# Stick-breaking mixer of a decoder trunk: projection with features on the partitions, and token factors on the scores

## The chip, the cores and the metric

The kernel runs on one core of a Trainium2 chip. The metric is the device time of one execution in microseconds, the median of three runs. TensorE (PE) does the matmuls and the transposes, VectorE (DVE), ScalarE (ACT) and GpSimd (POOL) the rest, and SyncE (SP) issues most DMAs. Inputs and outputs are fp32.

## The reference, cut to what matters

Two layers, 512 tokens, 1024 features. Each layer is half a feed-forward step, three token mixers A, B and C that share one input projection, gates and an output projection, and another half of a feed-forward step. The change lies in mixer C, which has six heads of 64 features:

```python
u = rms_norm(h, g_mix)
proj = u @ w_in
c = c_in.reshape(B, S, 3, C_HEADS, HEAD_DIM)             # query, key, value
o_c = stick_breaking_attention(c[:, :, 0], c[:, :, 1], c[:, :, 2])
...
z = einsum('bqhd,bshd->bhqs', qb, k) * dh ** -0.5
before = s_pos < tb                                       # strictly causal
log_1mb = where(before, log_sigmoid(-z), 0.0)
between = cumsum(log_1mb, axis=3, reverse=True) - log_1mb
a = where(before, exp(log_sigmoid(z) + between), 0.0)
o = einsum('bhqs,bshd->bqhd', a, vf)
```

The weight of a key is sigmoid(z) times the product of sigmoid(-z) over all keys between it and the query.

## The kernel before

**Numbers.** TensorE reads values in a rounded fp32 form (F32R). A value that must be exact is held as two such parts: `hi`, a copy by ScalarE that rounds, and `lo`, which VectorE gets by subtracting `hi` from the value. A product of two values is three matmuls: hi x hi, hi x lo and lo x hi. For the normalised input the parts are `gh` and `gl` (eight tiles of 128 features by 512 tokens each), for the weights `whi` and `wlo`. A transpose is a matmul with the identity `ident`, and runs in plain fp32.

**Normalisation.** `gh` and `gl` hold the input times the gain `g`, without the division by the root mean square, which belongs to the token. `rstd` computes that factor with tokens on the partitions: `r` (and `rq` = r/8, with the scale of the scores in it), a column per block of 128 tokens. `rbcast` spreads it over a tile `Rb` of 128 partitions by 512 tokens, for results that have features on the partitions. Both are called while the projection for the first pair of mixer C runs (`after`).

**The stream.** Weights go through the core as a sequence of jobs (`mix_jobs`, and `side_jobs` when the first has nothing ready). A job yields chunks: `fetch` starts the chunk's load on SP's queue and its splits in `wsplit` (L346-362: `raw` has three buffers, `whi` and `wlo` four), one chunk ahead of the one that `step` runs. Its `use` issues the matmuls into accumulator banks (`acc`, four banks).

**The units.** The attention work is cut into units: Python generators that yield the time after which they want to be resumed. `weave` keeps a model clock, to which every matmul and transpose adds its cost, resumes the units that are due and fills up with steps of the stream. So TensorE's queue, which keeps the order of the program, has projection matmuls with pieces of attention strewn in. On the other engines the scheduler of the framework may reorder what is ready.

**Mixer C.** Heads go in pairs (`p` = 0, 1, 2). `c_inputs` projects query, key and value of a pair: `project_in` with tokens on the partitions, four accumulators (one for each block of 128 tokens) of 384 columns (128 each for query, key and value), in four chunks of two K tiles. The stationary operand is the input, the moving one the weights. When a block is done, `evac` copies it out: `cq` (times `rq`), `ck` (times `r`, each head twice side by side, so that the transposes give it on both halves of the partitions), and `v_split` takes the value with its factor apart into `hi` and `lo`. `c_prep` is a unit that turns key and query round: for each head `k_dup` transposes four blocks of `ck` (tile `tps`) and splits the result in `kh` and `kl`; `q_stacks` transposes four blocks of `cq` and makes one tile `qs` per head, with the high part on one half of the partitions and the low part on the other. A score is then two matmuls (`scores`): `qs` against `kh` and against `kl`.

`c_unit` is one attention unit, half of a head's queries. Its `chain` goes from the scores (bank `sps`, one buffer): two sigmoids on ScalarE, of the scores for `e` and of their negative for `f`; a causal select on GpSimd after each; on VectorE a scan of `f` from the right with products; on GpSimd the product of `e` and the scanned `f`. After `chain.delay` TensorE transposes `e` (bank `tps`, two buffers) and it is split into `ph`/`pl` or `pzh`/`pzl`, and multiplied with the value's parts into the bank `ops`. The order in `mix_units` is: the preparation of pair 0, two units, the preparation of pair 1, two units, and so on; in the last pair the two of mixer B, `b_keys` and `b_compress`, take the place of a preparation.

Of the kernel before, what the change touches and what calls it, by code (L numbers as in the profile page):

```python
# [8 lines left out]
F32 = mybir.dt.float32  # L9
F32R = mybir.dt.float32r  # L10
I32 = mybir.dt.int32
AF = mybir.ActivationFunctionType
ALU = mybir.AluOpType
# [4 lines left out]
KD = D // 128  # L18
# [3 lines left out]
C_IN0 = A_IN + 512 + 768 + 24  # L22
# [33 lines left out]
class Trunk:  # L56
# [237 lines left out]
    def rstd(self, dil=False):  # L294

        nc = self.nc
        ps = self.tps()
        n = 8 if dil else 4
        ssd = self.ss.rearrange("p (m c) -> p c m", c=4)
        for j in range(n):  # L300
            rows = ssd[:, j - 4, :] if j > 3 else self.ss[:, j * 128:(j + 1) * 128]
            self.mm(ps[:, j:j + 1], rows, self.ones[:, 0:1], start=True, stop=True)
        tile_ = lambda name: self.rp.tile([128, 8], F32, tag=name, name=name, bufs=2)[:, :n]
        ms, r, t, rq = tile_("ms"), tile_("r"), tile_("rt"), tile_("rq")
        nc.vector.tensor_scalar(ms, ps[:, 0:n], 1.0 / D, EPS, op0=ALU.mult, op1=ALU.add)
        nc.scalar.activation(r, ms, AF.Sqrt)
        nc.vector.reciprocal(r, r)
        nc.vector.tensor_tensor(t, ms, r, op=ALU.mult)
        nc.vector.tensor_tensor(t, t, r, op=ALU.mult)
        nc.vector.tensor_scalar(t, t, -0.5, 1.5, op0=ALU.mult, op1=ALU.add)  # L310
        nc.vector.tensor_tensor(r, r, t, op=ALU.mult)
        if dil:
            nc.vector.tensor_scalar(rq, r, 0.125, None, op0=ALU.mult)
        self.r, self.rq = r, rq

    def rbcast(self):
# [375 lines left out]

    def q_stacks(self, view):

        nc = self.nc
        ps = self.trans4(view)
        out = []
        for h in range(2):
            t = self.st(F32R, "qs")
            own = slice(64 * h, 64 * h + 64)  # L700
            oth = slice(64 - 64 * h, 128 - 64 * h)
            nc.scalar.activation(t[own], ps[own], AF.Copy)
            nc.vector.tensor_tensor(t[oth], ps[own], t[own].bitcast(F32), op=ALU.subtract)
            out.append(t)
        return out
# [94 lines left out]


    def c_inputs(self, l, p):
        nc = self.nc
        c = self.cin[p] = {}

        def pre():
            if p == 0:
                self.begin_mix(l)
            elif p == 1:
                self.dilate()  # L810
            c["nq"] = self.mp.tile([128, 4, 128], F32, tag="oh", name="cq", bufs=5)
            c["nk"] = self.mp.tile([128, 4, 256], F32, tag="nat", name="ck", bufs=2)
            c["v"] = self.mp.tile([128, 4, 2, 128], F32R, tag="v2", name="v2", bufs=3)

        def evac(j, ps):
            r, rq = self.r[:, j:j + 1], self.rq[:, j:j + 1]
            nc.scalar.activation(c["nq"][:, j, :], ps[:, 0:128], AF.Copy, scale=rq)
            nc.scalar.activation(
                c["nk"][:, j, :].rearrange("p (h r d) -> p h r d", h=2, r=2),
                ps[:, 128:256].rearrange("p (h d) -> p h d", h=2)[:, :, None, :].to_broadcast([128, 2, 2, 64]),  # L820
                AF.Copy, scale=r)
            self.v_split(c["v"], j, ps[:, 256:384], 2, r)

        return self.project_in(l, [(C_IN0 + t * 384 + p * 128, 128) for t in range(3)], 2, False, evac, pre,
                               lambda: self.done.add(("c", l, p)),
                               after=(None, None, lambda: self.rstd(True), self.rbcast) if p == 0 else ())

    def c_prep(self, l, p):
        def make(U):
            c = self.cin[p]  # L830
            c["k"] = []
            yield "", 1300
            for h in range(2):
                c["k"].append(self.k_dup(lambda j: c["nk"][:, j, 128 * h:128 * h + 128]))
                yield "", 2000
                if h == 0:
                    c["q"] = self.q_stacks(lambda j: c["nq"][:, j, :])
                    yield "", 2000
            self.done.add(("cp", l, p))

        return Unit(make, need=lambda: ("c", l, p) in self.done)

    def c_unit(self, l, p, h, u):
        nc = self.nc

        def chain(i, S_, e):
            n = 128 * (i + 1)
            f = self.et("f")[:, :n]
            for t, sgn, fill in ((f, -1.0, 1.0), (e, 1.0, 0.0)):
                nc.scalar.activation(t, S_, AF.Sigmoid, scale=sgn)  # L850
                nc.gpsimd.affine_select(t[:, i * 128:], t[:, i * 128:], pattern=[[-1, 128]], compare_op=ALU.is_gt,
                                        fill=fill, base=0, channel_multiplier=1)
            nc.vector.tensor_tensor_scan(f[:, ::-1], f[:, ::-1], f[:, ::-1], 1.0, op0=ALU.mult, op1=ALU.min)
            nc.gpsimd.tensor_tensor(e[:, 0:n - 1], e[:, 0:n - 1], f[:, 1:n], op=ALU.mult)  # L854

        chain.delay = (4500, 4900)

        def make(U):
            c = self.cin[p]

            def first(O):
                if u == 0:
                    O["t"] = self.ops()
                    O["new"] = True

            def end(O):
                if u == 1:
                    if h == 0:
                        c["of"] = self.mp.tile([128, 512], F32, tag="of", name="of", bufs=1)
                    self.head_out(O["t"], h, c["of"])  # L870
                    O["free"] = self.clock + 2500
                    if h == 1:
                        self.oc.append(self.o_split(c["of"]))
                        self.done.add(("co", l, p))
                        if p == 2:
                            self.done.add(("cdone", l))

            yield from self.attend(U, u, c["q"][h], c["k"][h], chain, c["v"], h, self.O, u == 0, first, True, end)

        return Unit(make, need=lambda: ("cp", l, p) in self.done, gap=4500 if u else 3000, tiles=4 if u else 3,  # L880
                    pt=True)
# [844 lines left out]
```

## Time and profile before

| | value |
| --- | --- |
| median of three runs | 2807.02 us (2807.02, 2805.44, 2807.44) |
| the profiled execution | 2808.57 us, of which the span is 2806.9 us |
| granted TensorE clock, mean | 0.997 |
| PE busy | 2772.0 us, 99% |
| DVE busy | 1498.6 us, 53% |
| ACT busy | 1176.3 us, 42% |
| POOL busy | 486.2 us, 17% |
| DMA | 274.57 MB, mean 98 GB/s |

Matmuls overlap in the trace: a matmul of 512 columns has an entry of 0.39 us, and they start 0.23 us apart. Busy time of PE is therefore not the sum of its rows, and the cost of one more matmul is read from the distance of the starts. The chain of work that ended last shows this distance, since each of its pieces reaches to the start of the next. In the first layer mixer C's first query block (`cq`) is copied out at 398.4 us, in the second layer the last one at 1829.4 us.

### The profile page before, as it was taken

To read this page: it belongs to the slowest core of one execution; us is meant where nothing else is said; L and a number is where in the kernel's file an instruction comes from. 1 tells how busy PE (TensorE), PEld (TensorE's weight loads), DVE (VectorE), ACT (ScalarE), POOL (GpSimd) and SP (SyncE) were. 2 spreads that over 40 slices of the span, in tenths; PEclk is the share of its full clock that TensorE was granted. 3 is DMA by queue.
4 is the path that set the end of the run, shared out by engine and by line. 5 is a ranking of instruction groups with operands and counts; after the bars stand their busy time and mean duration, and the time that the engine had idled before them with its cause. 6 is when DMAs were issued, how large, how long until landed. Compare 5 with 4: busy or idle time off the path is not lost.

```text
span 2806.9 us, 39062 instructions
## 1 busy us (share of the span) xinstructions
PE 2772.0 (99%) x14281; PEld 2385.3 (85%) x14281; DVE 1498.6 (53%) x2983; ACT 1176.3 (42%) x2427; POOL 486.2 (17%) x577
## 2 busy tenths in 40 slices
PE   8999999999999999999999999999999999999998
PEld 7888898889989888888888888988899898888886
DVE  5464356567655674544354443565767456645433
ACT  4333246455644433333233332554656444433332
POOL 2121012122301231110011100221333012311100
PEclk9999999999999999999999999999999999999999
DMA  3332332332233243332333333323222333333332
GB/s 129 98 96 92 117 95 83 99 93 83 67 107 101 87 150 98 98 95 94 98 97 98 98 102 107 94 90 99 86 78 79 102 106 109 120 102 95 97 98 75
DMA packets 298575, 274.57 MB, mean 98 GB/s; under 512 B 14616, under 2 KB 278928, under 8 KB 298384
## 3 DMA queue, kind: packets, MB, share of 16 engines
q1 hardware_dynamic: 291744, 261.34, 30.6%
q10 hardware_dynamic: 6640, 10.75, 1.1%
q8 instruction: 112, 1.84, 0.3%
q14 instruction: 79, 0.65, 0.1%
HBM read 253.69 MB, written 18.35 MB: 97 GB/s over the span
## 4 chain that ended last, share of the span: by engine, by line
PE 95%; DVE 2%; issue 1%; POOL 1%; ACT 1%; DMA 0%; ACTq 0%; DVEq 0%; POOLq 0%
PE acc L82 66%; PE tps L82 9%; PE sps L82 8%; PE ops L82 8%; PE tps L102 4%; DVE wlo L359 0%; DMA gt<-gate 0%; POOL e L854 0%; POOL ss L292 0%; POOL ra L678 0%; DVE e L1227 0%; DMA gr<-in_cmp_pe_v_dram 0%; ACT e L1229 0%; PE acc L102 0%; DVE rb L679 0%
## 5 line engine op out<-in xcount | busy, mean ns | idle before, releaser
L359 DVE TENSOR_TENSOR wlo<-raw,whi 128x512 fp32r<-128x512 f32 (+3 forms) x944 | 650.4, 695 | 866.9 <-ACT whi L358 844.7
L358 ACT ACTIVATE whi<-raw 128x512 fp32r<-128x512 f32 (+3 forms) x944 | 561.5, 601 | 1043.6 <-PE acc L82 765.2
L82 PE MATMUL acc<-gh,whi 128*128 128x512 f32 x928 | 364.3, 393 | 0.0
L82 PE MATMUL acc<-gh,wlo 128*128 128x512 f32 x928 | 361.6, 390 | 0.0
L82 PE MATMUL acc<-gl,whi 128*128 128x512 f32 x928 | 361.4, 389 | 0.0
L530 POOL TENSOR_TENSOR a<-a,Rb 128x512 f32<-128x512 f32 x88 | 130.0, 1503 | 907.4 <-DVE a L529 893.5
L82 PE MATMUL acc<-hh,whi 128*128 128x512 f32 x704 | 274.2, 390 | 0.0
L82 PE MATMUL acc<-hh,wlo 128*128 128x512 f32 x704 | 273.9, 389 | 0.0
L82 PE MATMUL acc<-hl,whi 128*128 128x512 f32 x704 | 273.9, 389 | 0.0
L82 PEld LDWEIGHTS acc<-gh,wlo 128*128 128x128 f32 x928 | 174.1, 188 | 36.7
L82 PEld LDWEIGHTS acc<-gl,whi 128*128 128x128 f32 x928 | 174.4, 188 | 34.9
L82 PEld LDWEIGHTS acc<-gh,whi 128*128 128x128 f32 x928 | 174.4, 188 | 34.7
L82 PE MATMUL acc<-whi,gh 128*128 128x384 f32 (+2 forms) x576 | 203.1, 353 | 0.0
L82 PE MATMUL acc<-wlo,gh 128*128 128x384 f32 (+2 forms) x576 | 197.7, 343 | 0.5 <-DVE wlo L359 0.5
L82 PE MATMUL acc<-whi,gl 128*128 128x384 f32 (+2 forms) x576 | 197.2, 342 | 0.0
L82 PEld LDWEIGHTS acc<-hh,wlo 128*128 128x128 f32 x704 | 132.1, 188 | 27.5
L82 PEld LDWEIGHTS acc<-hh,whi 128*128 128x128 f32 x704 | 132.1, 188 | 27.4
L82 PEld LDWEIGHTS acc<-hl,whi 128*128 128x128 f32 x704 | 132.1, 188 | 27.1
L82 PE MATMUL acc<-whi,gd 128*128 128x384 f32 x384 | 134.6, 350 | 0.0
L82 PE MATMUL acc<-wlo,gd 128*128 128x384 f32 x384 | 129.3, 337 | 0.0
L82 PE MATMUL acc<-whi,gld 128*128 128x384 f32 x384 | 129.1, 336 | 0.0
L82 PE MATMUL tps<-gh,whi 128*128 128x512 f32 x320 | 124.5, 389 | 0.0
(377 smaller groups left out, 5412.6 us busy)
## 6 DMA issues: line engine op xcount, KB each, us to landing
raw<-in_ffn_w_dram SPq DMA_DIRECT2D x256, 512.0 KB, 3.4
raw<-in_w_in_dram SPq DMA_DIRECT2D x288, 128.0 KB, 2.3
raw<-in_w_gate_dram SPq DMA_DIRECT2D x48, 512.0 KB, 3.5
raw<-in_w_in_dram SPq DMA_DIRECT2D x16, 512.0 KB, 3.6
raw<-in_w_out_dram SPq DMA_DIRECT2D x16, 512.0 KB, 3.5
gate<-gt ACTq DMA_DIRECT2D x28, 256.0 KB, 2.0
gt<-gate SPq DMA_DIRECT2D x28, 256.0 KB, 2.8
raw<-in_w_up_dram SPq DMA_DIRECT2D x16, 384.0 KB, 3.0
```

Of the source, the lines that this page charges most:

```text
L82: self.nc.tensor.matmul(out, lhsT, rhs, start=start, stop=stop, **kw)
L102: self.nc.tensor.transpose(out, in_, self.ident[:n, :n])
L358: nc.scalar.activation(hi, x, AF.Copy)
L359: nc.vector.tensor_tensor(lo, x, hi.bitcast(F32), op=ALU.subtract)
L530: nc.gpsimd.tensor_tensor(v[j], v[j], self.Rb, op=ALU.mult)
```

## The change

Mixer C's projection puts the features on the partitions. The weights are now the stationary operand and `gh`/`gl` (512 tokens) the moving one; each pair has three accumulators of 512 columns, in the order value, query, key, in the same four chunks of two K tiles. All three go through the same chunks; value and query are finished and copied out a little ahead of the key.

- The query's accumulator already has the layout of `qs`: `stack_q` (the second half of the old `q_stacks`) splits it straight from the bank. It carries no factor.
- The key's accumulator is multiplied by `Rb` on VectorE into `ck` (in SBUF, 128 features by 512 tokens); `post` then writes `kh` and `kl` of each head on both halves of the partitions, four pairs of operations on 64 partitions, out of `ck`.
- The value is copied to `cv`; `c_prep` transposes its four blocks and calls `v_split` on them with `r`. That is all that `c_prep` still does.
- The query's factor stands now in the sigmoids: `scale` is a column, `rq` for `e`, and for `f` the new `nrq` = -r/8 that `rstd` computes.

```diff
--- before.py
+++ after.py
@@ -310,7 +310,9 @@
         nc.vector.tensor_scalar(t, t, -0.5, 1.5, op0=ALU.mult, op1=ALU.add)
         nc.vector.tensor_tensor(r, r, t, op=ALU.mult)
         if dil:
+            self.nrq = tile_("nrq")
             nc.vector.tensor_scalar(rq, r, 0.125, None, op0=ALU.mult)
+            nc.vector.tensor_scalar(self.nrq, r, -0.125, None, op0=ALU.mult)
         self.r, self.rq = r, rq
 
     def rbcast(self):
@@ -692,8 +694,10 @@
 
     def q_stacks(self, view):
 
-        nc = self.nc
-        ps = self.trans4(view)
+        return self.stack_q(self.trans4(view))
+
+    def stack_q(self, ps):
+        nc = self.nc
         out = []
         for h in range(2):
             t = self.st(F32R, "qs")
@@ -800,42 +804,81 @@
 
 
     def c_inputs(self, l, p):
+
         nc = self.nc
         c = self.cin[p] = {}
+        W = self.ins["w_in"][l]
+        starts = [C_IN0 + t * 384 + p * 128 for t in (2, 0, 1)]
+        after = {2: lambda: self.rstd(True), 3: self.rbcast} if p == 0 else {}
+        ps = []
 
         def pre():
             if p == 0:
                 self.begin_mix(l)
             elif p == 1:
                 self.dilate()
-            c["nq"] = self.mp.tile([128, 4, 128], F32, tag="oh", name="cq", bufs=5)
-            c["nk"] = self.mp.tile([128, 4, 256], F32, tag="nat", name="ck", bufs=2)
             c["v"] = self.mp.tile([128, 4, 2, 128], F32R, tag="v2", name="v2", bufs=3)
-
-        def evac(j, ps):
-            r, rq = self.r[:, j:j + 1], self.rq[:, j:j + 1]
-            nc.scalar.activation(c["nq"][:, j, :], ps[:, 0:128], AF.Copy, scale=rq)
-            nc.scalar.activation(
-                c["nk"][:, j, :].rearrange("p (h r d) -> p h r d", h=2, r=2),
-                ps[:, 128:256].rearrange("p (h d) -> p h d", h=2)[:, :, None, :].to_broadcast([128, 2, 2, 64]),
-                AF.Copy, scale=r)
-            self.v_split(c["v"], j, ps[:, 256:384], 2, r)
-
-        return self.project_in(l, [(C_IN0 + t * 384 + p * 128, 128) for t in range(3)], 2, False, evac, pre,
-                               lambda: self.done.add(("c", l, p)),
-                               after=(None, None, lambda: self.rstd(True), self.rbcast) if p == 0 else ())
+            c["vt"], kt = (self.mp.tile([128, 512], F32, tag="oh", name=n, bufs=5) for n in ("cv", "ck"))
+            return kt
+
+        def evac(j):
+            if j == 0:
+                nc.scalar.activation(c["vt"], ps[0], AF.Copy)
+            else:
+                c["q"] = self.stack_q(ps[1])
+
+        def post(kt):
+            nc.vector.tensor_tensor(kt, ps[2], self.Rb, op=ALU.mult)
+            c["k"] = []
+            for h in range(2):
+                own, oth = (slice(64 * x, 64 * x + 64) for x in (h, 1 - h))
+                hi, lo = self.st(F32R, "kh"), self.st(F32R, "kl")
+                for rows in (own, oth):
+                    nc.scalar.activation(hi[rows], kt[own], AF.Copy)
+                    nc.vector.tensor_tensor(lo[rows], kt[own], hi[own].bitcast(F32), op=ALU.subtract)
+                c["k"].append((hi, lo))
+            self.done.add(("c", l, p))
+
+        def entries():
+            kt = []
+            for ci in range(4):
+                def use(hi, lo, ci=ci):
+                    if ci == 0:
+                        kt.append(pre())
+                        ps.extend(self.acc() for _ in range(3))
+                    for j in range(3):
+                        cs = slice(j * 128, (j + 1) * 128)
+                        for k in range(2):
+                            g = 2 * ci + k
+                            self.mm(ps[j], hi[k][:, cs], self.gh[g], start=(g == 0), stop=False)
+                            self.mm(ps[j], hi[k][:, cs], self.gl[g], start=False, stop=False)
+                            self.mm(ps[j], lo[k][:, cs], self.gh[g], start=False, stop=(g == KD - 1))
+                            if k == 0:
+                                yield 0
+                        if ci == 3 and j < 2:
+                            evac(j)
+                        if j < 2:
+                            yield 0
+                    if ci in after:
+                        after[ci]()
+                    if ci == 3:
+                        post(kt[0])
+                    yield 1
+
+                rows = slice(ci * 256, ci * 256 + 256)
+                yield [(j * 128, 128, W[rows, c0:c0 + 128]) for j, c0 in enumerate(starts)], 2, 384, use
+
+        return None, entries()
 
     def c_prep(self, l, p):
+
         def make(U):
             c = self.cin[p]
-            c["k"] = []
             yield "", 1300
-            for h in range(2):
-                c["k"].append(self.k_dup(lambda j: c["nk"][:, j, 128 * h:128 * h + 128]))
-                yield "", 2000
-                if h == 0:
-                    c["q"] = self.q_stacks(lambda j: c["nq"][:, j, :])
-                    yield "", 2000
+            ps = self.trans4(lambda j: c["vt"][:, j * 128:(j + 1) * 128])
+            for j in range(4):
+                self.v_split(c["v"], j, ps[:, j * 128:(j + 1) * 128], 2, self.r[:, j:j + 1])
+            yield "", 2000
             self.done.add(("cp", l, p))
 
         return Unit(make, need=lambda: ("c", l, p) in self.done)
@@ -846,8 +889,8 @@
         def chain(i, S_, e):
             n = 128 * (i + 1)
             f = self.et("f")[:, :n]
-            for t, sgn, fill in ((f, -1.0, 1.0), (e, 1.0, 0.0)):
-                nc.scalar.activation(t, S_, AF.Sigmoid, scale=sgn)
+            for t, rq, fill in ((f, self.nrq, 1.0), (e, self.rq, 0.0)):
+                nc.scalar.activation(t, S_, AF.Sigmoid, scale=rq[:, i:i + 1])
                 nc.gpsimd.affine_select(t[:, i * 128:], t[:, i * 128:], pattern=[[-1, 128]], compare_op=ALU.is_gt,
                                         fill=fill, base=0, channel_multiplier=1)
             nc.vector.tensor_tensor_scan(f[:, ::-1], f[:, ::-1], f[:, ::-1], 1.0, op0=ALU.mult, op1=ALU.min)
```

Three places, as the engines' queues have them. First ScalarE, from the end of the projection of pair 0 in the first layer up to the first sigmoid of the first unit, which loads its table first. Before:

```order
L818 ACTIVATE ck<-acc,r 128x256
L725 ACTIVATE v_2977<-acc,r 128x2x64
L323 ACTIVATE Rb<-tps 128x512
L358 ACTIVATE whi<-raw 128x384 x2
L712 ACTIVATE kh<-tps 128x512
L358 ACTIVATE whi<-raw 128x384 x2
L702 ACTIVATE qs<-tps 64x512 x2
L712 ACTIVATE kh<-tps 128x512
L358 ACTIVATE whi<-raw 128x384 x2
L850 ACT_TABLE_LOAD
L850 ACTIVATE f<-sps 128x128
```

After (`cv` is the value's copy, `ck` the key in SBUF, `v_` the value's parts):

```order
L826 ACTIVATE cv<-acc 128x512
L706 ACTIVATE qs<-acc 64x512
L360 ACTIVATE whi<-raw 128x384 x2
L706 ACTIVATE qs<-acc 64x512
L325 ACTIVATE Rb<-tps 128x512
L837 ACTIVATE kh<-ck 64x512 x4
L729 ACTIVATE v_2975<-tps,r 128x2x64
L360 ACTIVATE whi<-raw 128x384 x2
L729 ACTIVATE v_2975<-tps,r 128x2x64 x2
L893 ACT_TABLE_LOAD
L893 ACTIVATE f<-sps,nrq 128x128
L729 ACTIVATE v_2975<-tps,r 128x2x64
```

The key's splits have moved from the preparation, where they came one head at a time between the weights' `whi`, into one row of four right behind `Rb`; the value's splits, which stood in the projection's end, are now between and behind the weights' `whi` and beside the first sigmoids.

Second VectorE, at the end of the projection of pair 1 (the two rows L853, after L896, are the scans of a unit of pair 0; `pzl` and `pl` are low parts of its transposed weights). Before:

```order
L853 SCALAR_TENSOR_TENSOR f<-f 128x384
L853 SCALAR_TENSOR_TENSOR f<-f 128x512
L359 TENSOR_TENSOR wlo<-raw,whi 128x384 x2
L713 TENSOR_TENSOR kl<-tps,kh 128x512
L766 TENSOR_TENSOR pzl<-tps,pzh 128x384
L359 TENSOR_TENSOR wlo<-raw,whi 128x384 x2
L703 TENSOR_TENSOR qs<-tps,qs 64x512
L766 TENSOR_TENSOR pl<-tps,ph 128x512
L703 TENSOR_TENSOR qs<-tps,qs 64x512
L713 TENSOR_TENSOR kl<-tps,kh 128x512
```

After:

```order
L896 SCALAR_TENSOR_TENSOR f<-f 128x384
L707 TENSOR_TENSOR qs<-acc,qs 64x512
L896 SCALAR_TENSOR_TENSOR f<-f 128x512
L831 TENSOR_TENSOR ck<-acc,Rb 128x512
L707 TENSOR_TENSOR qs<-acc,qs 64x512
L361 TENSOR_TENSOR wlo<-raw,whi 128x384
L838 TENSOR_TENSOR kl<-ck,kh 64x512 x4
L361 TENSOR_TENSOR wlo<-raw,whi 128x384
L730 SCALAR_TENSOR_TENSOR v_3167<-tps,r,v_3167 128x2x64
L770 TENSOR_TENSOR pzl<-tps,pzh 128x384
```

Behind the scan of 512 there now stand the product with `Rb` and half of the query's split, one `wlo`, and the four `kl` ahead of the next `wlo`; before, the scan of 512 was followed by two `wlo` at once, and `kl` and `qs` came one by one with other work between.

Third GpSimd, beside the unit `b_keys`, which runs in the last pair's units (`ra`, `natk` and `natq` belong to mixer B's rotary step). Before:

```order
L678 TENSOR_TENSOR ra<-natk,cos 128x256
L851 AFFINE_SELECT f<-f 128x128
L851 AFFINE_SELECT e<-e 128x128
L680 TENSOR_TENSOR natk<-ra,rb 128x16x8
L854 TENSOR_TENSOR e<-e,f 128x511
L678 TENSOR_TENSOR ra<-natq,cos 128x128 x2
```

After:

```order
L680 TENSOR_TENSOR ra<-natk,cos 128x256
L894 AFFINE_SELECT f<-f 128x128
L682 TENSOR_TENSOR natk<-ra,rb 128x16x8
L894 AFFINE_SELECT e<-e 128x128
L897 TENSOR_TENSOR e<-e,f 128x511
L680 TENSOR_TENSOR ra<-natq,cos 128x128 x2
```

The select of `e` has moved behind the step on `natk`.

TensorE's queue has 12,461 rows instead of 12,617. SP's queue has the same loads; two of mixer B's small ones have moved past one load of `raw`.

## The prediction

> **What bounds the kernel now.** I read the busy shares first, then the chain of work that ended last, then what TensorE waited for.
>
> ```profile
> PE 2772.0 (99%) x14281; PEld 2385.3 (85%) x14281; DVE 1498.6 (53%) x2983; ACT 1176.3 (42%) x2427; POOL 486.2 (17%) x577
> ...
> PE 95%; DVE 2%; issue 1%; POOL 1%; ACT 1%; DMA 0%; ACTq 0%; DVEq 0%; POOLq 0%
> ```
>
> TensorE is busy for 99% of the span and carries 95% of the chain; the others are about half idle or more. So a microsecond of TensorE work taken out of its queue is a microsecond off the end, and work on the others costs nothing until TensorE waits for it. How rare such waits are now stands in the view of waits of TensorE:
>
> ```profile
> PE tps L102 <- DMA gr<-in_cmp_pe_v_dram: 6.9, 1, 6.9
> PE sps L82 <- DVE sm L1227: 5.8, 8, 1.8
> ...
> PE tps L102 <- POOL e L854: 1.3, 2, 0.7
> ```
>
> The columns are microseconds, times, longest. None of these rows is a wait for a projection of mixer C or for its stacks; the one that mixer C owns is for GpSimd's last product `e`, 0.7 us once per layer. Two sums follow: what TensorE is spared, and what new waits the rearranged VectorE and ScalarE queues bring it.
>
> **Spared: wider matmuls.** A busy time of overlapped matmuls says little, so I take start-to-start time from the chain in order of time (start, length, what, count):
>
> ```profile
> 43.51 10.88 PE acc L82 x48
> ...
> 412.87 5.21 PE acc L82 x30
> ...
> 428.06 0.44 PE tps L102 x4
> ...
> 456.20 2.76 PE acc L82 x12
> ```
>
> The run of 30 is mixer C's projection, 384 columns: 5.21/30 = 173.7 ns each. The 48 are 512 columns in the feed-forward part: 10.88/48 = 226.7 ns. Per column that is 0.452 against 0.443 ns: both forms stream the same number of columns, and fewer, wider matmuls pay the fixed 13 ns less often. A pair of heads takes 8 K tiles x 4 token blocks x 3 products = 96 matmuls before, 8 x 3 outputs x 3 = 72 after: 16.67 against 16.32 us, 0.35 us spared. Six pairs (three in each of two layers): **2.1 us**. The weights are the same bytes in the same splits, so no DMA and no split is added; SP's queue only lets two compression weights pass one other load.
>
> **Spared: transposes.** The tiles' own view gives the counts:
>
> ```profile
> L102 PE MATMUL tps<-ident,ck x48: 270/272/322, 403.1 to 1868.8; 128*128 128x128 f32 x48
> ...
> L102 PE MATMUL tps<-ident,cq x24: 270/272/275, 406.1 to 1865.9; 128*128 128x128 f32 x24
> ```
>
> That is 18 groups of four; six groups (`cv`) remain. The row at 428.06 prices one group at 0.44 us of the chain, the pause before the next product included. 12 x 0.44 = **5.3 us**. Behind the last pair TensorE's queue holds the same rows as before, a few units of attention standing three matmuls earlier or later, so no later stage is rearranged. Spared in all: 7.4 us.
>
> **Added: operations off TensorE.** Prices from the groups kept apart by shape:
>
> ```profile
> L702 ACT ACTIVATE qs<-tps 64x512 fp32r<-64x512 f32 x28 | 16.6, 594 | 14.8 <-PE tps L102 10.5 <-DVE qs L703 3.8
> ...
> L1043 ACT ACTIVATE natk<-acc,r 128x256 f32<-128x256 f32 x16 | 7.7, 479 | 2.2 <-DVE glog L1042 2.2
> ...
> L850 ACT ACTIVATE e<-sps 128x256 f32<-128x256 f32 x12 | 4.8, 400 | 0.0
> ...
> L713 DVE TENSOR_TENSOR kl<-tps,kh 128x512 fp32r<-128x512 f32 x20 | 13.8, 690 | 7.3 <-ACT kh L712 6.9
> ...
> L853 DVE TENSOR_TENSOR_SCAN f<-f 128x512 f32<-128x512 f32 x12 | 15.1, 1261 | 6.5 <-POOL f L851 6.2
> ...
> L854 POOL TENSOR_TENSOR e<-e,f 128x511 f32<-128x511 f32 x12 | 14.8, 1231 | 7.7 <-DVE f L853 7.3
> ```
>
> The key now takes one product with `Rb` and four `kh`/`kl` pairs on half the partitions, where two full ones stood. Half the partitions save no time (`qs`, 64 rows: 594 ns), so VectorE gets 3 x 0.69 = 2.1 us more per pair and ScalarE two more `kh`. ScalarE loses twelve evacuations and gains `cv`; its load falls. The work is not more than these engines can carry; what matters is that it now stands in one lump at the end of each pair, ahead of weight splits and of the scan. The token factor as a per-token scale makes each of the 96 sigmoids longer: with such a scale 128x256 took 479 ns (`natk`), without 400; I take +0.09 us each. `nrq` is one tiny VectorE operation per layer (0.2 us, nothing waits).
>
> *End of pair 0.* Count from the start of its last K chunk. TensorE comes to transpose the first unit's `e` after 4.2 (18 matmuls), 0.8 (`Rb`), 2.0, 0.44 (`cv`), 2.7, 0.5 (scores), 5.4: at 16.1 us. ScalarE: `Rb` done at 5.9, `ck` on VectorE at 6.8, four `kh` to 9.0, a `v`, two weight tiles that wait for the chunk's end (10.2), two `v`, the 1.28 us table load (12.0), then `f` of 128, a `v`, `e`, and `f` of 256 at 12.75. Before, from that `f` to the end of the last product it took 2.82 us:
>
> ```profile
> 413.45 0.39 ACT L850 ACTIVATE f<-sps 128x256 f32<-128x256 f32 x1
> ...
> 415.63 0.64 POOL L854 TENSOR_TENSOR e<-e,f 128x255 f32<-128x255 f32 x1
> ```
>
> Now GpSimd does the first product ahead of the second select (+0.4) and the scale adds 0.09: ready at 16.05. TensorE had 1.6 us to spare here and has none. I take 0.2, between 0 and 1. The stacks themselves are in time: `kl` of head 0 at 8.9, scores at 10.3.
>
> *End of pair 1.* Count from the end of the query's matmuls. VectorE: the scan of 512 ends at 3.1, `ck` 3.8, second `qs` 4.45, `wlo` 5.0, four `kl` 7.6, the next chunk's second `wlo` 8.15. TensorE reaches that tile after 0.46 (scores), 1.36 (key), 2.72, 0.44, 0.68, 0.33, 0.68 and five more matmuls: 7.8. **0.35 late**; between 0 and 1.2. The accumulator that `qs` frees (4.5) is wanted at 4.9.
>
> *End of pair 2.* Count from its last matmul. The scan of 384 ends at 3.1, `wlo` 3.75, four `kl` 6.4, scan of 512 7.65, GpSimd's product 8.95. TensorE asks at 0.47 + 0.35 + 2.04 + 0.46 + 5.44 = 8.76. I take 0.3 with the scale; between 0 and 1.2.
>
> *The one existing wait*, in the unit that runs beside `b_keys`:
>
> ```profile
> 585.95 1.33 POOL L680 TENSOR_TENSOR natk<-ra,rb 128x128 f32<-128x128 f32 x1
> ...
> 587.25 1.13 POOL L854 TENSOR_TENSOR e<-e,f 128x511 f32<-128x511 f32 x1
> ...
> 588.43 0.55 PE L102 MATMUL tps<-ident,e 128*128 128x128 f32 x3 [0.66 <-POOL e L854]
> ```
>
> The `e` select now stands behind `natk` (0.29 us) and the sigmoids are longer, and nothing hides it: +0.3; between 0.1 and 0.6.
>
> That is 1.15 us per layer. A wait also costs TensorE its run-in:
>
> ```profile
> 389.67 0.34 PE L82 MATMUL acc<-whi,gl 128*128 128x384 f32 x1
> ...
> 390.27 0.44 PE L82 MATMUL acc<-wlo,gh 128*128 128x384 f32 x1 [0.27 <-DVE wlo L359]
> ```
>
> 0.27 us of wait here made 0.60 from start to start instead of 0.17, so 0.16 more; I put 0.05 per layer on top, as not all of the three will appear. **Two layers: 2.4 us lost**, bounds 0.2 and 8.
>
> **Sum.** -7.4 + 2.4 = -5.0 us. The profiled execution took 2808.57 us around a span of 2806.9; with the change 2803.6. The median of the runs is 2807.02, 1.55 below it, so I forecast 2802.0.
>
> **Rival 1: no new wait.** The three margins above are a few tenths; if the real operations overlap slightly better than I added, only the +0.3 beside `b_keys` stays, or nothing. -7.4 to -6.8: 2799.6 to 2800.2. For it: in the profile before, the same queues kept TensorE fed with 1.3 us of `e` waits in 48 units. Against: three lumps land exactly where the slack was.
>
> **Rival 2: slower, because `kl` and GpSimd shut each other out.** Before, `kl` read PSUM; now both its inputs are in SBUF, like those of `wlo`. What happens to such a pair beside GpSimd:
>
> ```profile
> 406.26 1.09 DVE L359 TENSOR_TENSOR wlo<-raw,whi 128x384 fp32r<-128x384 f32 x2 [1.19 <-ACT whi L358]
> ...
> 426.47 1.89 DVE L359 TENSOR_TENSOR wlo<-raw,whi 128x384 fp32r<-128x384 f32 x2
> ...
> 426.69 1.25 POOL L854 TENSOR_TENSOR e<-e,f 128x511 f32<-128x511 f32 x1 [1.23 <-DVE f L853]
> ...
> 587.36 2.44 DVE L359 TENSOR_TENSOR wlo<-raw,whi 128x512 fp32r<-128x512 f32 x2
> ```
>
> Alone the pair took 1.09 us, beside a GpSimd product 1.89; the worst pair of 512 took 2.44, 1.22 each. If all four `kl` cost that instead of 0.69, each end is 2.1 us later. At all six ends, with the +0.3 and the run-ins above: 2.4 x 6 + 0.6 = 15 lost, 2814.6. It decides from 1.2 us lost per end (break-even) and 2.2 (slower by 0.2%). In a mild form one `kl` of each pair stands behind one whole product of GpSimd, 1.25 us by the row at 426.69: 6 x 1.25 = 7.5 lost, about 2807 if no margin absorbs it. Against both: GpSimd works in short bursts of one unit, and by my count idles while pair 0's `kl` run.
>
> The Trainium skill ("SBUF — State Buffer", "Who interferes with whom") says that a VectorE operation with two SBUF inputs and a GpSimd operation that reads SBUF hold a shared port against each other for a whole instruction, and that operations with one SBUF input do not contend. The `wlo` rows agree with that (0.5 us alone against 0.9 beside a product); by that rule the mild form is the one to expect wherever a product of GpSimd falls on a `kl`, and no row yet shows `kl` from SBUF.
>
> **Chances.** What a measurement of this kernel can tell from no change is about 0.2%, 5.6 us. The forecast is some new waits, a gain of 1 to 6.5 us. The mild form of Rival 2, which eats the gain without making it measurably slower: 0.05. Rival 2 in full: 0.05. I put Rival 1 at 0.40 and the forecast at 0.50. So faster 0.40 (Rival 1 alone passes 2801.4), same 0.55, slower 0.05. The range runs from Rival 1 less the 1.6 us by which the lowest of the three runs lay under their median (2798.0) to the mild form (2807.0); the forecast's own is 2800.5 to 2806.0.
>
> **What would show it.** Right: 72 matmuls of 512 columns at 227 ns per pair, 24 `cv` transposes, PE's work 7 us less; new TensorE waits for `e`, `wlo` at 2.4 us in all; sigmoids of 256 columns at 490 ns. Wrong: TensorE waits for `kl` or `qs` at the scores (then the stacks, not their neighbours, are late); `kl` above 1 us (Rival 2); no new row of waits (Rival 1); or matmuls with weights as the stationary side slower than 227 ns in mixer C.

## The result, and the profile after

The changed kernel takes 2845.94 us (median of four runs, 2845.58 to 2846.22) against 2807.23 us for the kernel before (2805.44 to 2808.39): ratio 1.0133, 95% interval 1.0121 to 1.0145. It is 38.7 us slower. I had forecast 2802.0 us in a range from 2798 to 2807, and given slower a chance of 0.05.

The page of the changed kernel, in the lines that answer to those of before (span, busy shares, chain by engine):

```profile
span 2843.9 us, 38642 instructions
...
PE 2806.5 (99%) x14089; PEld 2363.1 (83%) x14089; DVE 1506.4 (53%) x3003; ACT 1183.1 (42%) x2397; POOL 489.7 (17%) x577
...
PE 95%; DVE 2%; ACT 1%; POOL 1%; issue 1%; DMA 0%; DVEq 0%; SPq 0%; POOLq 0%; ACTq 0%
```

TensorE has 192 instructions fewer and is busy 34.5 us longer. Its waits do not explain that: the rows of the view of waits that are new or longer (`e` had 1.3 us before, the other two nothing) add 4.7 us:

```profile
PE tps L102 <- POOL e L897: 3.7, 6, 1.0
PE sps L82 <- ACT e L893: 1.6, 4, 0.6
...
PE tps L102 <- DVE pzl L770: 0.7, 2, 0.3
```

So the matmuls themselves must be slower, and not only mixer C's. The chain in order of time shows it 60 us into the program, in the first feed-forward part, more than 300 us ahead of mixer C:

```profile
66.73 11.20 PE acc L82 x48
...
89.13 11.20 PE acc L82 x48
```

48 matmuls of 512 columns take 11.20 us where they took 10.88 (the row at 43.51 in the prediction): 233.3 ns from start to start instead of 226.7. The groups by shape say which matmuls these are. Before, and then after:

```profile
L82 PE MATMUL acc<-hh,whi 128*128 128x512 f32 x704 | 274.2, 390 | 0.0
L82 PE MATMUL tps<-gh,whi 128*128 128x512 f32 x320 | 124.5, 389 | 0.0
```

```profile
L82 PE MATMUL acc<-hh,whi 128*128 128x512 f32 x704 | 274.3, 390 | 0.0
L82 PE MATMUL tps<-gh,whi 128*128 128x512 f32 x320 | 126.6, 396 | 0.0
```

Where `hh` is streamed past the weights nothing has changed; where `gh` (or `gl`) is, each matmul is longer. Work, shapes and weights are alike. It is no throttle: by stretches of time, the granted clock was 1.00 in both kernels while one began 443 matmuls in 100 us and the other 430. The stretch from 100 to 200 us, before and then after (PE, PEld, DVE, ACT, POOL busy, clock, DMA share, GB/s):

```profile
100.00:200.00 100.00, 100.00 (x443) 82.79 (x442) 57.98 (x127) 35.27 (x59) 21.59 (x25) 1.00 0.33 100
```

```profile
100.00:200.00 100.00, 100.00 (x430) 80.59 (x429) 56.48 (x125) 34.52 (x58) 21.88 (x25) 1.00 0.31 90
```

What the change does touch in that stage is the place of tiles. `nrq` is a new tile of 32 bytes per partition with two buffers, in the pool `rp`. That pool lies in front of the pool `wp`, so `raw`, `whi`, `wlo` and every tile of the later pools (`hh`, `gd`, all of mixer C) move by 64 bytes; `gh` and `gl`, in the pool `gp` ahead of it, stay. The distance follows from the sizes of the tiles in `kernel.py`: between the first `gh` and the first `whi` lie eight `gh` and eight `gl` (32768 bytes per partition), the pool `rp` (8448 before, 8512 after) and three `raw` (12288). So `whi` begins 53504 bytes behind `gh` before and 53568 after.

### The profile page after: what moved, and what is told of

The parts are those of the page before. It is cut to its first block, busy times and chain, and to the rows that moved or that the text cites. A ratio compares the mean times of both kernels' runs of the same rounds, so it can differ in the third digit from the quotient of the medians.

```text
span 2843.9 us, 38642 instructions
## 1 busy us (share of the span) xinstructions
PE 2806.5 (99%) x14089; PEld 2363.1 (83%) x14089; DVE 1506.4 (53%) x3003; ACT 1183.1 (42%) x2397; POOL 489.7 (17%) x577
## 4 chain that ended last, share of the span: by engine, by line
PE 95%; DVE 2%; ACT 1%; POOL 1%; issue 1%; DMA 0%; DVEq 0%; SPq 0%; POOLq 0%; ACTq 0%
PE acc L82 66%; PE tps L82 9%; PE sps L82 8%; PE ops L82 8%; PE tps L102 4%; DVE wlo L361 0%; POOL e L897 0%; POOL ss L292 0%; ACT whi L360 0%; ACT e L1272 0%; DVE f L896 0%; DVE rb L681 0%; DVE e L1270 0%; DMA x<-in_x_dram 0%; PE acc L102 0%
## 5 line engine op out<-in xcount | busy, mean ns | idle before, releaser
L82 PE MATMUL acc<-gh,whi 128*128 128x512 f32 x1072 | 429.4, 401 | 0.0
L82 PE MATMUL acc<-gh,wlo 128*128 128x512 f32 x1072 | 425.0, 396 | 0.1
L82 PE MATMUL acc<-gl,whi 128*128 128x512 f32 x1072 | 424.7, 396 | 0.0
L82 PEld LDWEIGHTS acc<-gh,wlo 128*128 128x128 f32 x1072 | 202.1, 188 | 50.6 <-DVE wlo L361 1.7
L82 PEld LDWEIGHTS acc<-gl,whi 128*128 128x128 f32 x1072 | 202.4, 189 | 46.0
L82 PEld LDWEIGHTS acc<-gh,whi 128*128 128x128 f32 x1072 | 202.3, 189 | 46.0
L82 PE MATMUL acc<-whi,gh 128*128 128x384 f32 (+2 forms) x384 | 136.5, 356 | 0.0
L82 PE MATMUL acc<-wlo,gh 128*128 128x384 f32 (+2 forms) x384 | 133.5, 348 | 0.0
L82 PE MATMUL acc<-whi,gl 128*128 128x384 f32 (+2 forms) x384 | 133.2, 347 | 0.0
```

The source lines that it names most:

```text
L82: self.nc.tensor.matmul(out, lhsT, rhs, start=start, stop=stop, **kw)
```

## Experiments on the place of the tiles

In the first seven kernels no instruction differs from the kernel they start from, in kind, shape or order on the four engines; only unused bytes are allocated, or a pool is created earlier. The edit for those with unused bytes, here with 64:

```diff
         self.wp = pool("wp", bufs=2)
+        self.rp.tile([128, 16], F32, tag="pad", name="pad", bufs=1)
```

and for the kernel that moves `gh` and `gl` along with the weights:

```diff
-        self.gp = pool("gp", bufs=8)
         self.rp = pool("rp", bufs=2)
+        self.gp = pool("gp", bufs=8)
```

**The kernel before with 64 unused bytes** (before_pad64).

> The kernel before, with 64 unused bytes per partition behind the small tiles of the pool rp, so that raw, whi, wlo and all that is allocated behind them lie 64 bytes further, as they do in the changed kernel; no instruction differs. Address theory (a matmul that streams gh, gl, yh or yl is slower by 6.6 ns when the weight tiles lie 64 bytes off their former place): 3 x 1632 + 384 = 5280 such matmuls, +35 us, about 2842. Rival (the new projection or what it does to the engines slows the stages around it): 2807, as before.

Measured: 2843.37 us, ratio 1.0127 (1.0110 to 1.0144) to the kernel before. The same 48 matmuls in its chain:

```profile
110.00 11.20 PE acc L83 x48
```

That is the loss without any of the change's work: 35.0 us against the 2808.37 us of the kernel before beside it, where the 432 more such matmuls of the changed kernel would add 2.9. The theory that the new code slows its surroundings has fallen.

**The changed kernel with rp ahead of gp** (after_rp_first).

> The changed kernel with the pool rp allocated ahead of gp, so that gh and gl move by 64 bytes (modulo 128) together with whi and wlo; no instruction differs. Address theory with the distance between the streamed tile and the weights deciding: 2808. Address theory with the place of the weights alone deciding: 2846. Rival (the new code): 2846.

Measured: 2809.48 us, ratio 1.0006 (0.9996 to 1.0015). The 48 matmuls:

```profile
109.13 10.88 PE acc L82 x48
```

Of the 38.7 us, 1.1 are left (against 2808.37 us for the kernel before beside it). It is the distance between the streamed tile and the weights that counts, not the place of either: here `whi` stays where the changed kernel has it and `gh` moves, and in before_pad64 `whi` moves and `gh` stays.

**The changed kernel with 64 and with 32 more unused bytes** (after_pad64, after_pad32).

> The changed kernel, with another 64 unused bytes in the pool rp, so that raw, whi, wlo lie 128 bytes behind their place in the kernel before; no instruction differs from the changed kernel. Address theory: 3 x 1776 + 384 = 5712 matmuls lose their 6.6 ns, -37.7 us, 2808; the forecast of 2802 would then be 6 us short of it by new waits in mixer C. Rival (the new code slows the rest): 2846, as the changed kernel.

> The changed kernel with 32 more unused bytes: the weight tiles lie 96 bytes behind their place in the kernel before. Address theory, if only the half of a 128-byte line counts in which a tile starts: 96 is in the other half, 2846. If any distance off a multiple of 128 counts: 2846 too. If only a distance of exactly 64 counts: 2808. Rival (the new code): 2846.

Measured: 2842.89 us (1.0124, 1.0109 to 1.0139) and 2852.13 us (1.0156, 1.0141 to 1.0171). Here my theory of 128-byte lines missed: 128 bytes off the old place is nearly as slow as 64, and 96 is slower still, 6 us beyond what any of the three theories gave. The chain has 11.16 us for 48 matmuls with 128 bytes and 11.25 with 96:

```profile
109.73 11.16 PE acc L83 x48
```

```profile
110.94 11.25 PE acc L83 x48
```

Looking at the addresses again: before, `whi` and `gh` differ by 256 modulo 512, and so does every K tile's weight block, since blocks of 128 columns stand 512 bytes apart; with rp first they differ by 0. `hh` lies at the same distance from `whi` in all of these kernels, as both lie behind the pad, and was never slow (226 to 227 ns). So both 0 and 256 are good places, and a period of 256 bytes was the next theory.

**The kernel before with 32, 192 and 256 unused bytes** (a single run each).

> The kernel before, with 32 unused bytes in the pool rp. Modulo 256, the weight tiles then start 32 bytes behind the tiles gh and gl that are streamed past them. Theory of the 256-byte period (a streamed tile and the stationary tiles must start at the same place modulo 256, else a matmul of 512 columns takes 5 to 7 ns longer, whatever the distance): 5280 matmuls x 5 to 7 ns, 2833 to 2845. Rival (only distances of 64 and more count, as of a 64-byte word): 2808.

> The kernel before, with 192 unused bytes in the pool rp: the distance is 192 modulo 256, which is 64 short of the period. Theory of the 256-byte period, with a slowdown that depends on the distance to the nearest multiple: as with 64 bytes, 2843. Rival (the period is 64 or 128 and other tiles made the difference): 2808.

> The kernel before, with 256 unused bytes in the pool rp. Theory of the 256-byte period: a matmul takes 226.7 ns again, 2808. Rival (every place but the first one and the one with equal addresses modulo 512 is slow): 2843.

Measured: 2842.65, 2825.14 and 2808.48 us, beside 2808.02 for the kernel before. With 256 the matmul is back at 226.7 ns; with 192 it is at 229.0:

```profile
109.05 10.88 PE acc L83 x48
```

```profile
109.94 10.99 PE acc L83 x48
```

The period holds. That the loss depends on the distance to the nearest multiple does not: 64 on one side costs 6.7 ns per matmul, 64 on the other 2.3. All places together, the distance from `gh` to `whi` modulo 256 against the run of 48 matmuls:

| distance | 48 matmuls, us | kernel |
| --- | --- | --- |
| 0 | 10.88 | before, before_pad256, after_rp_first |
| 32 | 11.20 | before_pad32 |
| 64 | 11.20 | after, before_pad64 |
| 96 | 11.25 | after_pad32 |
| 128 | 11.16 | after_pad64 |
| 192 | 10.99 | before_pad192 |

**Which tiles decide** (a single run each). In the first kernel `wlo` alone is 64 bytes off, in the second `whi` alone, in the third `gl` alone, and the others agree modulo 256 (in the first, `hh` and `hl` agree with `wlo` and not with `whi`). The pads, each allocated once:

```diff
 # before_wlo64, in wtiles, ahead of wlo
+self.wp.tile([128, 16], F32, tag="pad", name="pad", bufs=1)
 # before_whi64: 64 unused bytes in rp, and in wtiles, ahead of wlo
+self.wp.tile([128, 48], F32, tag="pad", name="pad", bufs=1)
 # before_gl64, in scaled, ahead of gl and behind it
+self.gp.tile([128, 48], F32, tag="pa", name="pa", bufs=1)
+self.gp.tile([128, 16], F32, tag="pb", name="pb", bufs=1)
```

> The kernel before, with 64 unused bytes between whi and wlo, so that whi keeps its place and wlo moves by 64. TensorE's order in a K tile is gh with whi, gl with whi, gh with wlo. If a matmul is slowed by its own stationary tile's place, the start-to-start time after gh with wlo grows to 233 ns and the other two stay at 227: 5280 / 3 x 6.6 = 12 us, 2820. If it is slowed by the load of the next weights, which runs beside it, the time after gl with whi grows instead, by the same 12 us. If both, 23 us.

> The kernel before, with whi moved by 64 bytes and wlo and all behind it by 256: modulo 256, gh and gl (and hh, hl in the other matrix) start at the place of wlo and 64 bytes off whi. When wlo was the one that was off, the start-to-start time after gh with wlo was 236 ns (9 more) and after the other two 228 to 229. If a matmul's own pair of tiles decides, the times after gh with whi and gl with whi grow now, by 6 to 9 ns each, and hh and hl with whi too: (1632 + 704) x 2 matmuls, 28 to 42 us, 2836 to 2850. If what is loaded beside a running matmul decides, the time after gh with wlo (beside which the next whi is loaded) and after gh with whi grows, gl with whi stays.

> The kernel before, with gl alone 64 bytes off the weights (modulo 256); gh, hh, hl, whi and wlo agree. If the place of the streamed tile against the weights decides for each matmul by itself, the time after gl with whi grows by 6 to 9 ns and the others stay: 1632 x 6 to 9 and 128 for yl: 11 to 16 us, 2819 to 2824. If the places of the streamed tiles did not matter and only where the weights stand did: 2808.

Measured: 2835.26, 2856.72 and 2822.63 us, the first two beyond what any theory gave. The medians of the start-to-start times over 1632 matmuls of each kind, worked out from the starts in the traces:

| ns after | all agree | `wlo` off | `whi` off | `gl` off |
| --- | --- | --- | --- | --- |
| `gh` with `whi` | 227 | 228 | 234 | 229 |
| `gl` with `whi` | 227 | 229 | 233 | 229 |
| `gh` with `wlo` | 227 | 236 | 234 | 228 |

Neither simple rule fits. That 2822.63 lies in the range of the first theory for `gl` is luck: the time after `gl` with `whi` grew by 2 ns, not by 6 to 9, and the other two grew as well. A matmul whose own two tiles agree can be slow (`gh` with `wlo` at 234 when `whi` is off: there the next weights, loaded beside it, are off), and one whose own tiles do not agree can be nearly undisturbed (`gl` with `whi`, 229 in the last column). What is shown is that the loss is nil when all agree modulo 256, and lies between about 5 and 23 ns for three matmuls otherwise. The rule inside stays open.

One rival can be settled from the starts in the same traces: that the streamed reads collide with the traffic of the other engines, which write `whi` and `wlo`, or with the loads into `raw`. With `wlo` off, the matmuls during which ScalarE, VectorE and GpSimd were idle and no DMA packet of the core was under way have the same medians as all others: 236 ns after `gh` with `wlo` (155 of them), 228 after `gh` with `whi` (162), 229 after `gl` with `whi` (112). So the loss does not come from them.

## Experiments on mixer C

With the tiles in place the change is worth nothing: 2809.48 against 2808.37 us. I had put 7.4 us of spared TensorE work against 2.4 us of new waits. The waits of TensorE in that kernel, from 380 to 546 us (mixer C of the first layer; before, this stretch had one row, 0.3 us for `wlo`):

```profile
PE tps L102 <- POOL e L897: 1.1, 2, 0.6
PE sps L82 <- ACT e L893: 0.6, 1, 0.6
PE acc L82 <- DVE wlo L361: 0.4, 2, 0.2
PE tps L102 <- DVE pzl L770: 0.3, 1, 0.3
```

A wait costs more than the view shows, as matmuls run in again behind it. By the starts of TensorE's instructions, the distances beyond the usual ones sum to 0.7 us at the end of pair 0, 1.0 at that of pair 1 and 1.55 at that of pair 2; in the unit beside `b_keys` the wait grew from 0.66 to 1.17 us. That is 3.75 us per layer, 7.5 in all: the whole gain. The end of pair 2, in the chain in order of time:

```profile
443.03 0.58 ACT f L893
443.61 0.52 ACT kh L837
...
444.14 0.63 ACT kh L837
...
444.79 0.59 ACT e L893
...
445.42 0.73 PE sps L82 x2
```

`f` and `e` are the two sigmoids of one score bank. Two `kh` stood between them on ScalarE, so the bank came free 1.2 us later, and TensorE's next scores waited. The scan and GpSimd's product behind them were late in turn. So the lump is the suspect, rather than the length of one operation.

**The lump taken apart** (spread): `post` only multiplies the key by `Rb`; the four pairs of `kh` and `kl` go into the preparation unit.

```diff
         def post(kt):
             nc.vector.tensor_tensor(kt, ps[2], self.Rb, op=ALU.mult)
+            c["kt"] = kt
...
-            c["k"] = []
-            for h in range(2):
-                ...
     def c_prep(self, l, p):
...
             yield "", 2000
+            for h in range(2):
+                ...                              # the same lines
+                yield "", 2000
```

> The changed kernel with rp ahead of gp (2809.5 when it ran), and with the four kh/kl pairs of a pair of heads moved from the end of the projection into the preparation unit, one head at a time with 2 us of the model clock between. The trace of the kernel without this move has TensorE lose 0.7 us at the end of pair 0, 1.0 at the end of pair 1 and 1.6 at the end of pair 2, in each layer. Theory of the lump (the four kh and kl stand ahead of scans and of the sigmoid that frees the score bank): the losses of pairs 1 and 2 go, 2 x 2.6 = 5 us, 2804. Rival (the waits come from the longer sigmoids and from one-buffer banks): 2809, no change.

Measured: 2803.72 us, ratio 0.9986 (0.9977 to 0.9995), 4 us faster than the kernel before. The waits of TensorE from 380 to 546 us are now:

```profile
PE tps L102 <- POOL e L901: 0.5, 1, 0.5
PE tps L102 <- ACT natc L1086: 0.4, 1, 0.4
PE acc L82 <- DVE wlo L361: 0.2, 1, 0.2
```

(The row of `natc` belongs to mixer B and stood just outside the stretch before.) And on ScalarE the sigmoids of pair 2 stand together again:

```profile
447.31 0.58 ACT L897 ACTIVATE f<-sps,nrq 128x384 f32<-128x384 f32 x1 [0.42 <-PE sps L82]
447.79 0.57 ACT L897 ACTIVATE e<-sps,rq 128x384 f32<-128x384 f32 x1
```

**The sigmoids with a constant scale** (plain_scale), on the kernel with rp first.

```diff
-            for t, rq, fill in ((f, self.nrq, 1.0), (e, self.rq, 0.0)):
-                nc.scalar.activation(t, S_, AF.Sigmoid, scale=rq[:, i:i + 1])
+            for t, rq, fill in ((f, -0.125, 1.0), (e, 0.125, 0.0)):
+                nc.scalar.activation(t, S_, AF.Sigmoid, scale=rq)
```

> The changed kernel with rp ahead of gp, and with the constant 0.125 as the scale of the sigmoids in place of the column of token factors: the query's token factor is left out of the result. Theory of the longer sigmoids (each took 0.085 us more with a column): the three chains that are on the path per layer get 0.2 to 0.35 us shorter each, -1 to -2 us, 2807.5 to 2808.5. Theory of the lump: it stays, so no more than that.

The kernel leaves the query's factor out. Measured: 2806.30 us, ratio 0.9992 (0.9983 to 1.0001). By the ratios that is 1.4 per mille under the kernel with the column, some 4 us, more than either theory allowed, though the two intervals overlap. The trace shows that more than the length changed: the order on ScalarE is another, and in pair 2 the first two `kh` now stand behind `e`.

```profile
443.27 0.49 ACT L893 ACTIVATE f<-sps 128x384 f32<-128x384 f32 x1
443.66 0.48 ACT L893 ACTIVATE e<-sps 128x384 f32<-128x384 f32 x1
444.03 1.28 ACT L837 ACTIVATE kh<-ck 64x512 fp32r<-64x512 f32 x2
```

So this run does not separate the price of the scale (0.58 us against 0.49 for a sigmoid of 384 columns, as forecast) from the order; it fits the lump, but does not show it.

**Both** (spread_qrb, spread_qrb2): as in spread, and VectorE also multiplies the query by `Rb`, so that the sigmoids have the constant scale of the last diff while the query's factor stays in. The first does the query's stacks in a stage of their own, the second without one.

```diff
+            nc.vector.tensor_tensor(c["qt"], ps[1], self.Rb, op=ALU.mult)
...
     def c_prep(self, l, p):
...
+            c["q"] = self.stack_q(c["qt"])
+            yield "", 2000                       # in the first alone
```

> The kernel spread, and the query multiplied by Rb on VectorE (one more operation of 0.69 us per pair) and stacked in the preparation unit, so that the sigmoids have a constant scale again and the factor is in the query as before. If the spread alone takes the waits away, this adds nothing: 2804. If the column scale is what is left of them, it is 1 to 2 us faster than spread: 2802 to 2803.

> The kernel spread_qrb without the extra stage of its preparation unit: TensorE's queue is that of spread, row for row, and the sigmoids have a constant scale. In spread_qrb the extra stage shifted the units and mixer A waited 1.95 us per layer for nata; in spread TensorE still waited 0.53 us per layer for e in pair 1 and 1.15 in the unit beside b_keys, where spread_qrb waited 0 and 0.68. If the waits are as these traces have them: 2803.7 - 2 x 1.0 = 2801.7. Rival (the extra 0.69 us of VectorE per pair brings another wait): 2804.

Measured: 2805.09 us (0.9989, 0.9981 to 0.9998) and 2803.31 us (0.9981, 0.9972 to 0.9990). The first missed: mixer C's new waits were gone, and 300 us later, in mixer A, another appeared, 1.95 us in each layer. The added stage had shifted the units against the stream, and without it (spread_qrb2) this row is gone:

```profile
PE tps L102 <- DVE nata L683: 3.9, 2, 1.9
```

The second has TensorE's queue row for row as in spread. It has the lowest median here, 5.3 us under the kernel before by the ratio; against spread its interval overlaps, so the two are not told apart, and its time lies between its two expectations. Its profiled execution, with a span of 2800.1 us, is near the lowest of its eleven; there mixer C's new waits are 0.6 us for `pzl` and 0.2 us for `e` in the first layer.

## Why the prediction was wrong

**The step that failed** was the sentence on `nrq`: "one tiny VectorE operation per layer (0.2 us, nothing waits)", together with "no later stage is rearranged". I priced the tile as an instruction and not as 64 bytes of memory in front of the weights. Nothing in my sum, nor in either rival, reached the feed-forward part. In its place: 5712 matmuls (1776 each of `gh` with `whi`, `gl` with `whi` and `gh` with `wlo`, and 384 of the output projection's pairs) at 0.32/48 us = 6.7 ns make 38.1 us, against 38.7 measured; with the tiles put right 1.1 us of the loss was left. One of the signs that I had named for being wrong did show, mixer C's own matmuls at 4.20/18 us = 233 ns in the chain of the changed kernel, but for the place of the tiles and not for the weights' being the stationary side:

```profile
428.74 4.20 PE acc L82 x18
```

**The spared work was right.** In the changed kernel the matmuls with `whi` and `wlo` as the stationary tiles went up from 1632 to 1776 of each kind, which is 72 per pair, and 24 transposes of `cv` are left. With the tiles in place they run at 226.7 ns, so the stationary side costs nothing of its own. The kernels spread and spread_qrb2, whose waits are nearest to those of before, come out 4 and 5 us faster, where 7.4 less what is left of the waits was due; the intervals (1 to 6 and 3 to 8 us) allow that, and do not show the 7.4 to the tenth.

**The new waits were mis-sized**: 1.2 us per layer forecast, 3.75 measured (first layer, tiles in place). End of pair 0: 0.2 forecast, 0.7 measured, by the chain that I counted (ScalarE, GpSimd, scan, product). End of pair 1: 0.35 against 1.0; beside the late `wlo`, `pzl` came late behind the four `kl`, which I had not followed. End of pair 2: 0.3 against 1.55, outside my bound of 1.2; I had counted VectorE's lump and not that `kh` could come between two sigmoids of one bank. Beside `b_keys`: 0.3 against 0.5. The places were right, the sizes were not, since I added durations in the order of the queues and left out what each late piece delays next.

**Rival 1** (no new wait) was wrong for this order of work. spread_qrb2 comes nearest to it, with 5.3 us gained where Rival 1 gave 6.8 to 7.4. The 48 units that it speaks of are 48 chains, two to a unit.

**Rival 2** (`kl` and GpSimd exclude each other) is right as a mechanism and small here. Of 24 `kl`, 22 took 0.68 to 0.69 us and two, the first of pair 2 in each layer, took 1.26. In the kernel with rp first, VectorE and GpSimd at that place:

```profile
445.96 1.26 DVE L838 TENSOR_TENSOR kl<-ck,kh 64x512 fp32r<-64x512 f32 x1 [0.40 <-PE sps L82]
```

```profile
445.81 0.86 POOL L897 TENSOR_TENSOR e<-e,f 128x383 f32<-128x383 f32 x1
```

GpSimd's product ran until 446.67, and the `kl` ended 0.55 us behind it. This agrees with the rule of the Trainium skill cited in the prediction ("SBUF — State Buffer", "Who interferes with whom"). It cost 0.57 us twice, and the 22 others overlapped no product, so it is a part of pair 2's lateness and not the cause of the 38.7 us. In the spread kernels more `kl` met a product: four of 24 took 1.2 to 1.5 us in spread and eight in spread_qrb2, and these are the two fastest kernels.

## What to carry to other kernels

A new tile is also a shift of every tile allocated behind it: compare the addresses of streamed and stationary tiles before and after, and keep the distances, as the pool created ahead of both did here. A pool of their own for small tiles, behind the large ones, or a pad up to the next 256 bytes should do the same; neither was run on the changed kernel. When a change moves the time, look first at the pitch of matmuls in a stage that it does not touch; if it is another there, the cause is not in the edited code. And work that is moved off a busy engine in one lump delays what stands behind it in the queue: the same operations, a head at a time in a unit of their own, took 5 to 6 us off (ratio 0.9986 against 1.0006).

## What the hardware showed that I had not expected

In this kernel the streams of `gh`, `gl`, `hh` and `hl`, fp32r matmuls of 512 columns, each with new weights, run at 226.7 ns from start to start if the streamed tiles and the stationary tiles begin at the same place modulo 256 bytes, and at 229 to 234 ns in the runs of 48 otherwise (tables above), at the same granted clock. With 384 columns and the weights streamed, the medians of each kind were 173 to 174 ns in the kernels whose tiles agree, and 173 to 179 in the others. The Trainium skill ("SBUF — State Buffer", "Who interferes with whom") gives TensorE two independent read ports, one for the streamed operand and one for weights, and says that TensorE never waits on another engine. The runs do not speak against the second: the loss was there too while ScalarE, VectorE, GpSimd and the DMAs were idle. But the price of a matmul depends on the distance of its two kinds of tiles, so for time the two reads do not behave as independent here; the measurement decides. How the places interact, and why 192 costs less than 64, was not settled.
